# Low parts of two of the seven sum forms of g by a negative copy and an accumulating DMA, in the second FFN block of a float32 decoder step

## The chip, the cores and the metric

The kernel runs on one core of one Trainium2 chip. The metric is the device time of one execution in microseconds (us). All data are float32. A matmul here takes operands that are rounded to a shorter float format (fp32r), so every operand is cut into two parts, a high part (the rounded value) and a low part (the value minus its high part), and each product is built from three matmuls: high by high, high by low and low by high.

## What is computed

One step of a decoder block on 520 tokens (512 of a new sequence, 8 single-token samples): a SwiGLU FFN with half weight, a mixer (pooling and a state-space scan), a second SwiGLU FFN with half weight, and a final norm. The change lies in the second FFN alone:

```python
def _swiglu(x, wg, wu, wd):
    return (jax.nn.silu(x @ wg) * (x @ wu)) @ wd
...
    h = h + 0.5 * _swiglu(_rms_norm(h, ffn2_norm[l]), ffn2_w_gate[l], ffn2_w_up[l], ffn2_w_down[l])
```

The model width is 1024, the FFN width 2816, so the hidden vector g = silu(gate) * up has 22 tiles of 128 rows.

## The kernel before

**Tiles and products.** The FFN block is `class Ffn`. Both its matrix products, gate and up on one side and down on the other, are done as 2x2 block products with seven block multiplications in place of eight. The two token halves (260 tokens each) are one side of the blocks. Each of the seven forms of an input (sums and differences of its blocks, "slots" 0 to 6) is held as high and low part. One tile `f` of gate and up is one turn of seven products (`product(f, p)`), each of 12 matmuls: per 128-row piece one matmul with the high and one with the low part of the input against the high weight, and at the end four against the low weight (`mm_low_last`). So a turn has 84 matmuls.

**Where g goes.** The first 16 tiles of g are taken in pairs (0,1), (2,3), ... (14,15). When the odd tile of a pair is done, `keep_g` makes the seven forms of the pair in the tile `gs` (128 x 2 x 7 x 260, high parts in `gs[:,0]`, low parts in `gs[:,1]`) from `xg` (the four blocks, tile `gq`) and `xd` (two differences, which lie in the scratch `acc_f`). `part(hi, lo, s)` makes a cut: ScalarE casts to the high part, VectorE subtracts for the low part. Slots 0 to 2 come from `xg`, slots 3 and 4 from `xd` (the 128 x 520 cut in question), slots 5 and 6 from `xg` again after a further difference.

**Turns of the down weights.** After eight tiles of g there are four turns with down weights, `Down(c, d)` with d = 0 to 3: c = 0 follows tile 8 and uses pairs 0 to 3, c = 1 follows tile 16 and uses pairs 4 to 7. Their products read the forms in `gs`. A turn's products stand in the order 1, (product 4 of the turn before), 5, 6, 3, 7, 2. Product 1 reads slot 0, product 5 reads slot 3, product 7 slot 4. Each goes through the four pairs in order. The last pair that a Down turn needs, tiles (6,7) or (14,15), is closed one turn ahead of it, in the turn of tile 8 or 16.

**Low parts by DMA.** A second way to a low part already exists, `part_by_dma`: ScalarE casts to the high part, ScalarE writes the negative of the high part into the low part's place, and a DMA from the GpSimd queue adds the source to it. It is used for the low half-weights `wlo` and, by the table `LOW_BY_DMA`, for the last quarter of some tiles' up weights (`qs`). The other tiles' quarters are cut by VectorE.

**Order.** TensorE's order is pinned by hand. On the other engines a planner with a simulated timeline sets the order when the program is built, and each engine then runs its list in order. Weights come in by SyncE's DMA queue (`raw`, two pairs of 128 x 1024 buffers, one pair per turn). The GpSimd queue carries the accumulating DMAs and, between them, the 16 sample states (`br` and `room` in, `out_nss` out), whose update is done by ScalarE (`so`) and VectorE (`room`) in tiles 6 and 17 to 21 and in the Down turns.

In `product`, the copy of the first product's result out of PSUM into `BE` (ScalarE, L504) stands ahead of product 5, which writes the other half of the same `BE`.

Of the kernel before, what the change touches and what calls it, by code (L numbers as in the profile page):

```python
# [10 lines left out]
F32 = mybir.dt.float32  # L11
F32R = mybir.dt.float32r
AF = mybir.ActivationFunctionType
# [27 lines left out]
QUARTERS = slice(0, HB // 2), slice(HB // 2, HB)  # L41
STATES = ((1, 1, 1, 1), (6, 17, 19, 20, 21), 4)
OUT_LOW_BY_DMA = ((1, 0), (1, 1))
LOW_BY_DMA = {1: (2, 3, 4, 5, 6), 2: (*range(7), 9, 11)}

CONV_PLAN = (
    "b0 b1 d0 b2 b3 x0 x1 v0 d1 x2 x3 d2 X0 p0 y0 c0 A0 k0 p1 x4 m0 x5 B0 c1 p2 m1 A1 x6 c2 A2 B1 x7 X1 m2 A3"
# [21 lines left out]
def tile_trunk_step(ctx: ExitStack, tc: tile.TileContext, ins: dict, outs: dict):  # L69
    nc = tc.nc  # L70
# [172 lines left out]
                                              op1=ALU.subtract)  # L243

    def part_by_dma(hi, lo, s, home):
        nc.scalar.copy(hi, s)
        nc.scalar.activation(out=lo, in_=hi.bitcast(F32), func=AF.Copy, scale=-1.0)
        nc.gpsimd.dma_start(out=lo, in_=home, accum_op=ALU.add)

    def part(hi, lo, s):  # L250
        cast = nc.scalar.copy(hi, s)
        low = nc.vector.tensor_tensor(out=lo, in0=s, in1=hi.bitcast(F32), op=ALU.subtract)  # L252
        return cast.ins, low.ins
# [17 lines left out]
    class Ffn:  # L271
# [72 lines left out]
        def keep_g(self, f, tg):  # L344
            if f >= self.folded:
                if not self.few:
                    self.few = self.cells(f"g{self.i}_{f}")
                g = self.g[f] = self.few.pop().rearrange("p (a b) t -> p a b t", a=2)
                self.closed = part(g[:, 0], g[:, 1], tg)
                return  # L350
            self.g[f] = tg
            if f % 2:
                gs = self.gs[f // 2] = self.new_gs(f"gs{f}")
                xg, xd = self.pairs[f - 1], self.nx[2].rearrange("p (b t) -> p b t", b=2)
                nc.vector.tensor_tensor(out=xd, in0=xg[:, 0::2], in1=xg[:, 3:4].to_broadcast([P, 2, HB]),
                                        op=ALU.subtract)
                nc.vector.scalar_tensor_tensor(out=xg[:, 3], in0=xd[:, 1], scalar=-1.0, in1=xg[:, 0], op0=ALU.mult,
                                               op1=ALU.subtract)
                part(gs[:, 0, 0:3], gs[:, 1, 0:3], xg[:, 0:3])
                part(gs[:, 0, 3:5], gs[:, 1, 3:5], xd)  # L360
                nc.vector.scalar_tensor_tensor(out=xg[:, 2], in0=xg[:, 3], scalar=-1.0, in1=xg[:, 1], op0=ALU.mult,
                                               op1=ALU.subtract)
                part(gs[:, 0, 5:7], gs[:, 1, 5:7], xg[:, 2:4])
# [90 lines left out]
        def quarter(self, f):  # L454
            src = self.held[f]
            n = f"{self.i}_{f}b"
            if self.qs is None:
                hi, lo = (self.wx.tile([P, 512], F32R, tag=t, name=f"{t}_{n}") for t in ("qhi", "qlo"))
            else:
                hi, lo = self.qs[0][:, :512], self.qs[0][:, 512:]  # L460
            h, l = hi, lo
            if len(src.shape) == 3:
                h, l = (t.rearrange("p (j c) -> p j c", j=4) for t in (hi, lo))
            if f in LOW_BY_DMA[self.i] and (f, 1) not in LOW_ON_DVE:
                part_by_dma(h, l, src, self.dram[f][1][:, 512:])
            else:
                part(h, l, src)
            self.w[f][4] = (hi, lo), range(4)
# [1024 lines left out]
```

## Time and profile before

| | |
|---|---|
| time, median of 3 runs | 951.61 us (951.32 to 952.19) |
| the profiled execution | 952.73 us, of which the span on the core is 950.9 us |
| TensorE matmul / weight load busy | 941.6 us (99%) / 923.9 us (97%) |
| VectorE busy | 851.8 us (90%) |
| ScalarE busy | 635.7 us (67%) |
| GpSimd busy | 152.6 us (16%) |
| second block: tiles 1 to 21 and the eight Down turns | about 612 to 900 us of the span |

The span is the time from the first to the last instruction on the core; the profiled execution is 1.1 us slower than the median. Lines of the trace give a start in us from the span's start, a duration in us, the engine, the source line and the operation with its output and inputs. PE is TensorE, PEld its weight loads, DVE VectorE, ACT ScalarE, POOL GpSimd, SP SyncE; "POOLq" and "SPq" are their DMA queues. "Us to landing" of a DMA runs from its issue to the moment that its completion is signalled.

### The profile page before, as it was taken

Reading aid. Unit: us, or ns where it says so; the run is one execution under the profiler, and the core shown is the slowest. Engines: PE = TensorE matmul, PEld = TensorE weight load, DVE = VectorE, ACT = ScalarE, POOL = GpSimd, SP = SyncE. Lnnn points to the kernel's source line nnn. Section 1 sums busy time; section 2 is a strip of 40 time slices with the busy share of each in tenths; the row PEclk is TensorE's granted clock in tenths of the full one; section 3 lists DMA queues with packets and bytes.
Section 4 is the critical chain, followed back from the end, with each engine's and each line's share of the span. In section 5 each row is a group of like instructions: output and inputs, shape, how many; then the busy total and the mean of one; then the engine's idle time right before and its main releaser. Section 6 shows DMA issues by size and latency. Waiting matters only on the chain. (4 is left out here: it accounts for less than half of the span.)

```text
span 950.9 us, 19685 instructions
## 1 busy us (share of the span) xinstructions
PE 941.6 (99%) x7674; PEld 923.9 (97%) x7674; DVE 851.8 (90%) x1462; ACT 635.7 (67%) x1178; POOL 152.6 (16%) x230
## 2 busy tenths in 40 slices
PE   9999999999999999999999999999999999999996
PEld 8999999999999999999999899999999999999996
DVE  6899899998988698779998998999999999999986
ACT  7777756667566465475768745777776677766764
POOL 0011100100100002146251100111112101122120
PEclk9999999999999999999999999999999999999998
DMA  7666554455553335354364443546666655767642
GB/s 212 180 164 146 148 147 140 113 135 164 134 153 97 87 96 162 91 169 150 97 179 133 140 113 117 139 120 156 164 178 175 164 147 137 172 203 181 171 158 91
DMA packets 54123, 138.36 MB, mean 146 GB/s; under 512 B 7878, under 2 KB 16006, under 8 KB 54030
## 3 DMA queue, kind: packets, MB, share of 16 engines
q1 hardware_dynamic: 40046, 104.20, 34.6%
q0 software_dynamic: 13712, 32.78, 18.6%
q8 instruction: 60, 0.98, 0.4%
q14 instruction: 33, 0.27, 0.1%
q10 hardware_dynamic: 272, 0.13, 0.0%
HBM read 129.74 MB, written 7.34 MB: 144 GB/s over the span
## 5 line engine op out<-in xcount | busy, mean ns | idle before, releaser
L504 ACT COPY ac<-A 128x260 f32<-128x260 f32 x85 | 31.7, 373 | 34.6 <-PE A L165 16.4
L433 DVE TENSOR_TENSOR s<-raw 128x1024 f32<-128x1024 f32 x39 | 47.6, 1221 | 4.0 <-DMA raw<-in_w2gu 2.5
L504 ACT COPY ac<-BE 128x260 f32<-128x260 f32 x41 | 15.5, 377 | 33.4 <-PE BE L165 17.6
L151 PE MATMUL inx<-xh_mx,whi_inx 128*128 128x260 f32 x112 | 31.8, 284 | 0.0
L154 PE MATMUL inx<-xl_mx,whi_inx 128*128 128x260 f32 x112 | 31.6, 282 | 0.0
L155 PE MATMUL inx<-xh_mx,wlo_inx 128*128 128x260 f32 x112 | 31.6, 282 | 0.0
L1033 DVE SCALAR_TENSOR_TENSOR A<-U,h,A 128x544 f32<-128x544 f32 x36 | 28.4, 789 | 1.8 <-ACT A L1031 1.4
L311 PE MATMUL P<-x,raw 128*128 128x260 f32 x128 | 29.3, 390 | 0.0
L311 PEld LDWEIGHTS P<-x,raw 128*128 128x128 f32 x128 | 24.9, 196 | 3.9
L160 PE MATMUL wo<-catg,whi_wo 128*128 128x260 f32 x192 | 27.4, 285 | 0.0
L160 PEld LDWEIGHTS wo<-catg,whi_wo 128*128 128x128 f32 x192 | 24.8, 188 | 0.2
L139 ACT CAST thi<-raw 128x1024 fp32r<-128x1024 f32 (+1 forms) x14 | 14.2, 1014 | 15.5 <-PE wo L160 4.8
L1311 DVE TENSOR_TENSOR h<-wo,h 128x260 f32<-128x260 f32 x48 | 19.2, 423 | 4.9 <-PE wo L165 4.7
L1199 ACT ACTIVATE so<-br,sxdt 128x128 f32<-128x128 f32 x64 | 22.7, 375 | 1.2 <-DVE room L1201 0.7
L252 DVE TENSOR_TENSOR gs<-gq,gs 128x780 fp32r<-128x780 f32 (+1 forms) x28 | 23.2, 829 | 0.0
L151 PE MATMUL inz<-xh_mx,whi_inz 128*128 128x260 f32 x80 | 22.9, 287 | 0.0
L154 PE MATMUL inz<-xl_mx,whi_inz 128*128 128x260 f32 x80 | 22.7, 283 | 0.0
L155 PE MATMUL inz<-xh_mx,wlo_inz 128*128 128x260 f32 x80 | 22.6, 283 | 0.0
L512 DVE TENSOR_TENSOR BE<-BE,ac 128x260 f32<-128x260 f32 (+1 forms) x41 | 18.5, 451 | 3.1 <-PE BE L155 1.7
L151 PEld LDWEIGHTS inx<-xh_mx,whi_inx 128*128 128x128 f32 x112 | 21.1, 188 | 0.2 <-issue 0.2
L160 PE MATMUL A<-xth_f,qs 128*128 128x260 f32 x84 | 21.2, 283 | 0.0
L160 PE MATMUL A<-xtl_f,qs 128*128 128x260 f32 x84 | 21.2, 284 | 0.0
(3135 smaller groups left out, 4380.9 us busy)
## 6 DMA issues: line engine op xcount, KB each, us to landing
raw<-in_w2gu SPq DMA_DIRECT2D x44, 512.0 KB, 4.3
raw<-in_w1gu SPq DMA_DIRECT2D x41, 512.0 KB, 4.2
raw<-in_w_in SPq DMA_DIRECT2D x24, 512.0 KB, 3.6
raw<-in_w1d SPq DMA_DIRECT2D x16, 512.0 KB, 4.6
raw<-in_w2d SPq DMA_DIRECT2D x16, 512.0 KB, 4.3
raw<-in_w_out SPq DMA_DIRECT2D x12, 512.0 KB, 3.5
ab<-scr_acs SPq DMA_DIRECT2D x8, 512.0 KB, 6.3
h<-in_state_ssm SPq DMA_DIRECT2D x16, 256.0 KB, 3.7
```

The source lines that it names most:

```text
L151: first = nc.tensor.matmul(ps, whi, xhi, start=start, stop=False, **kw)
L154: nc.tensor.matmul(ps, whi, xlo, start=False, stop=False, **kw)
L155: nc.tensor.matmul(ps, wlo, xhi, start=False, stop=stop, **kw)
L160: mm = nc.tensor.matmul(ps, w, x, start=start, stop=False, **kw)
L252: low = nc.vector.tensor_tensor(out=lo, in0=s, in1=hi.bitcast(F32), op=ALU.subtract)
L311: mm = nc.tensor.matmul(self.banks[f, u][b][:, :HB], ws(self.raw[f][:, u], j + 4 * q), xg[:, slot[q]], start=j == q == 0, stop=j == 3 and ...
L433: nc.vector.tensor_tensor(out=s1, in0=diag, in1=up0, op=ALU.add)
L504: self.copied = nc.scalar.copy(keep, out[:, :HB]).ins
L512: nc.vector.tensor_tensor(out=be[:, s], in0=be[:, s], in1=a[:, s], op=ALU.add)
L1033: nc.vector.scalar_tensor_tensor(out=A[:, :n], in0=U[:, j : j + n], scalar=w(j), in1=A[:, :n], op0=ALU.mult, op1=ALU.add)
L1199: nc.scalar.activation(out=o[:, q], in_=br, func=AF.Copy, scale=sxdt[:, j, b : b + 1]))
L1311: rows.append(nc.vector.tensor_tensor(out=h[:, d, hs], in0=ps[:, :HB], in1=h[:, d, hs], op=ALU.add).ins)
```

## The change

```diff
-LOW_BY_DMA = {1: (2, 3, 4, 5, 6), 2: (*range(7), 9, 11)}
+LOW_BY_DMA = {1: (2, 3, 4, 5, 6), 2: (0, 1, 2, 3)}
...
     def part_by_dma(hi, lo, s, home):
-        nc.scalar.copy(hi, s)
-        nc.scalar.activation(out=lo, in_=hi.bitcast(F32), func=AF.Copy, scale=-1.0)
+        cast = nc.scalar.copy(hi, s)
+        low = nc.scalar.activation(out=lo, in_=hi.bitcast(F32), func=AF.Copy, scale=-1.0)
         nc.gpsimd.dma_start(out=lo, in_=home, accum_op=ALU.add)
+        return cast.ins, low.ins
...
                 part(gs[:, 0, 0:3], gs[:, 1, 0:3], xg[:, 0:3])
-                part(gs[:, 0, 3:5], gs[:, 1, 3:5], xd)
+                if self.i == 2:
+                    part_by_dma(gs[:, 0, 3:5], gs[:, 1, 3:5], xd, xd)
+                else:
+                    part(gs[:, 0, 3:5], gs[:, 1, 3:5], xd)
```

In the second block, slots 3 and 4 of each of the eight pairs get their low part by the negative copy on ScalarE and an accumulating DMA of 128 x 520 from `acc_f` in SBUF; VectorE's eight subtractions go. In return the last quarters of tiles 4, 5, 6, 9 and 11 (the new tuple drops all five, tiles 4 and 5 among them) are cut by VectorE and no longer by negative copy and DMA. In all VectorE has three instructions fewer, ScalarE three more, GpSimd's queue three DMAs more. TensorE's and SyncE's rows are the same ones in the same order. Line numbers from 247 on are higher by one in the new file, from 361 on by four.

The planner also places neighbours anew. On ScalarE the negative copies do not stand right behind their casts. This is ScalarE before, from the cast of slots 3 and 4 of pair (6,7) to the first copy of the turn Down(0,0); L396 casts the next turn's weights, L397 makes their negative copy:

```order
L251 CAST gs_8550<-acc_f_7244 128x520
L139 CAST shi_Down(c=0, d=0)d<-raw 128x1024
L504 COPY ac_8_1_8506<-A_8_8503 128x260
L1199 ACTIVATE so_8616<-br_8227,sxdt 128x128
L396 CAST whi_Down(c=0, d=1)a<-raw 128x1024
L251 CAST gs_8550<-gq_6_8427 128x520
L504 COPY BE_Down(c=0, d=0)_8646<-A_Down(c=0, d=0)_8645 128x260
L397 ACTIVATE wlo_Down(c=0, d=1)a<-whi_Down(c=0, d=1)a 128x1024
```

And ScalarE now, at the same place:

```order
L246 CAST gs_8550<-acc_f_7244 128x520
L139 CAST shi_Down(c=0, d=0)d<-raw 128x1024
L508 COPY ac_8_1_8506<-A_8_8503 128x260
L1203 ACTIVATE so_8617<-br_8227,sxdt 128x128
L247 ACTIVATE gs_8550<-gs_8550 128x520
L400 CAST whi_Down(c=0, d=1)a<-raw 128x1024
L252 CAST gs_8550<-gq_6_8427 128x520
L508 COPY BE_Down(c=0, d=0)_8647<-A_Down(c=0, d=0)_8646 128x260
L401 ACTIVATE wlo_Down(c=0, d=1)a<-whi_Down(c=0, d=1)a 128x1024
```

The negative copy (L247) stands three instructions behind its cast, between `so` and the cast of the next turn's weights. The same holds at Down(1,0).

On GpSimd's queue, before, from the low weights of tile 8 to those of Down(0,2):

```order
L398 DMA wlo_8a<-in_w2gu 128x512
L1179 DMA br_8613<-scr_bc 128x128
L1180 DMA room<-in_state_ssm 128x512
L398 DMA wlo_Down(c=0, d=0)a<-in_w2d 128x1024
L398 DMA wlo_Down(c=0, d=1)a<-in_w2d 128x1024
L1179 DMA br_8749<-scr_bc 128x128
L398 DMA wlo_Down(c=0, d=2)a<-in_w2d 128x1024
L1203 DMA out_nss<-room 128x512
```

And now:

```order
L402 DMA wlo_8a<-in_w2gu 128x512
L402 DMA wlo_Down(c=0, d=0)a<-in_w2d 128x1024
L248 DMA gs_8550<-acc_f_7244 128x520
L1183 DMA br_8614<-scr_bc 128x128
L1184 DMA room<-in_state_ssm 128x512
L402 DMA wlo_Down(c=0, d=1)a<-in_w2d 128x1024
L1183 DMA br_8750<-scr_bc 128x128
L1207 DMA out_nss<-room 128x512
L402 DMA wlo_Down(c=0, d=2)a<-in_w2d 128x1024
```

The new DMA stands ahead of a state's two loads, which have moved from in front of Down(0,0)'s low weights to behind it, so three transfers now come between Down(0,0)'s and Down(0,1)'s low weights. `out_nss` and Down(0,2)'s low weights have changed places. GpSimd's queue at Down(1,0) to Down(1,2) is altered in the same way.

## The prediction

> **What bounds the kernel now.** First the page's first part:
>
> ```profile
> span 950.9 us, 19685 instructions
> PE 941.6 (99%) x7674; PEld 923.9 (97%) x7674; DVE 851.8 (90%) x1462; ACT 635.7 (67%) x1178; POOL 152.6 (16%) x230
> ```
>
> TensorE leaves 1% of the span. Then the busy times in stretches of the second block (columns: stretch, length, then busy us and count of PE, PEld, DVE, ACT, POOL, the granted clock, DMA share, GB/s):
>
> ```profile
> 640.00:670.00 30.00, 30.00 (x250) 29.80 (x249) 27.49 (x43) 22.05 (x38) 6.31 (x8) 1.00 0.69 163
> 780.00:820.00 40.00, 40.00 (x334) 39.92 (x334) 38.12 (x61) 29.63 (x51) 4.60 (x6) 1.00 0.58 147
> ```
>
> TensorE never pauses long enough to be seen here, its clock is full, and VectorE at 92 to 95% only keeps step. A busy PE may still hide short gaps, so I read the chain that ended last:
>
> ```profile
> 771.34 0.97 PE A L160 x8
> 781.42 0.97 PE A L160 x8
> ```
>
> The same product of tiles 13 and 14 lies 10.08 us apart, which is 84 matmuls at 0.12 us. I went through the starts of all weight loads from tile 2 to the last Down turn in this way: only two gaps stand out, of 0.27 and 0.15 us. The first:
>
> ```profile
> 665.19 0.19 PEld L160 LDWEIGHTS A<-xtl_f,qs 128*128 128x128 f32 x1
> 665.58 0.54 PEld L165 LDWEIGHTS A<-xth_f,qs 128*128 128x128 f32 x4 [0.20 <-DMA qs<-in_w2gu]
> ```
>
> 0.39 us in place of 0.12: TensorE waited for the low quarter of tile 6 from an accumulating DMA. So the second block is bound by TensorE's own rate. Relief of VectorE can bring at most these 0.42 us there, but whatever makes TensorE wait is added to the end nearly one for one, since no slack follows in which to catch up.
>
> **The new wait.** The readers of slots 3 and 4 decide. For most pairs they come a turn or more later; for the last pair ahead of each Down group they come at once, in product 5:
>
> ```profile
> 696.35 1.03 PEld L160 LDWEIGHTS BE_Down(c=0, d=0)_8646<-gs,shi_Down(c=0, d=0)c 128*128 128x128 f32 x8
> 697.31 0.19 PEld L165 LDWEIGHTS BE_Down(c=0, d=0)_8646<-gs,slo_Down(c=0, d=0)c 128*128 128x128 f32 x1
> 817.29 1.02 PEld L160 LDWEIGHTS BE_Down(c=1, d=0)_10189<-gs,shi_Down(c=1, d=0)c 128*128 128x128 f32 x8
> 818.24 0.55 PEld L165 LDWEIGHTS BE_Down(c=1, d=0)_10189<-gs,slo_Down(c=1, d=0)c 128*128 128x128 f32 x4
> ```
>
> The eight loads take the pieces in order, high then low, so the eighth needs the low part of slot 3 of the last pair: at 696.35 + 7 x 0.12 = 697.19, and at 817.29 + 0.83 = 818.12. Before, VectorE had it ready long ago:
>
> ```profile
> 693.23 0.70 DVE L252 TENSOR_TENSOR gs<-acc_f,gs 128x520 fp32r<-128x520 f32 x1
> ```
>
> 693.93 leaves 3.3 us. Now it goes by ScalarE and GpSimd. ScalarE's rows there, for c = 0 and then c = 1:
>
> ```profile
> 693.35 0.37 ACT L1199 ACTIVATE so<-br,sxdt 128x128 f32<-128x128 f32 x1
> 693.66 1.05 ACT L396 CAST whi_Down(c=0, d=1)a<-raw 128x1024 fp32r<-128x1024 f32 x1
> 695.24 0.36 ACT L504 COPY BE_Down(c=0, d=0)_8646<-A_Down(c=0, d=0)_8645 128x260 f32<-128x260 f32 x1
> ...
> 814.43 1.05 ACT L396 CAST whi_Down(c=1, d=1)a<-raw 128x1024 fp32r<-128x1024 f32 x1
> 816.86 0.38 ACT L504 COPY BE_Down(c=1, d=0)_10189<-A_Down(c=1, d=0)_10188 128x260 f32<-128x260 f32 x1
> ```
>
> ScalarE runs without a pause here, so the negative copy behind `so` starts where the cast L396 started, at 693.66 and 814.43. Its length I take from the same operation on `qs`, and the step from ScalarE to GpSimd from tile 5:
>
> ```profile
> L247 ACT ACTIVATE qs<-qs 128x512 fp32r<-128x512 f32 x7 | 4.5, 636 | 0.2
> ...
> 643.64 0.64 ACT L397 ACTIVATE wlo_5a<-whi_5a 128x512 fp32r<-128x512 f32 x1
> ...
> 644.57 0.85 POOL L398 DMA_DIRECT2D wlo_5a<-in_w2gu  x1 [6.23 <-ACT wlo_5a L397]
> ```
>
> 0.64 us, and 644.28 to 644.57, 0.29 us. The DMA is issued at 693.66 + 0.64 + 0.29 = 694.59 and at 815.36; GpSimd is free at both places. With L for the time to landing, TensorE waits 694.59 + L - 697.19 = L - 2.60 at Down(0,0). At Down(1,0) I first take away the second gap of the trace: product 5 began at 817.29 because the copy into `BE` ended at 817.24; the new order puts that copy ahead of the 1.06 us negative copy of the weights and only the 0.64 us one of `gs` is new ahead of it, so it ends earlier and the gap of 0.15 goes. The need is then 817.97 and the wait L - 2.61.
>
> **What L is.** No accumulating DMA of before has its source in SBUF. The nearest rows are those from GpSimd's queue of nearly the same size (256 KB against 260; last column us to landing):
>
> ```profile
> qs<-in_w2gu POOLq DMA_DIRECT2D x7, 256.0 KB, 7.0
> ...
> out_nss<-hs POOLq DMA_DIRECT2D x3, 256.0 KB, 2.3
> ...
> wlo_5a<-in_w2gu POOLq DMA_DIRECT2D x1, 256.0 KB, 3.8
> ...
> wlo_7a<-in_w2gu POOLq DMA_DIRECT2D x1, 256.0 KB, 6.9
> wlo_8a<-in_w2gu POOLq DMA_DIRECT2D x1, 256.0 KB, 4.5
> ```
>
> The lower bound is 2.3, a plain copy out of SBUF; the upper one 7.0, an accumulate in a crowd. In between the neighbours decide. What else moves counts, so here are the raw loads that follow (SPq), first behind tile 5's issue at 644.57 above, then behind tile 8's, then at the two new places:
>
> ```profile
> 646.10 20.87 SPq L389 DMA_DIRECT2D raw<-in_w2gu  x6
> ...
> 675.56 0.85 POOL L398 DMA_DIRECT2D wlo_8a<-in_w2gu  x1 [7.11 <-ACT BE L504]
> ...
> 676.32 0.33 SPq L389 DMA_DIRECT2D raw<-in_w2d  x1
> ...
> 695.09 0.33 SPq L389 DMA_DIRECT2D raw<-in_w2d  x1
> ...
> 815.86 0.33 SPq L389 DMA_DIRECT2D raw<-in_w2d  x1
> ```
>
> Tile 5's 3.8 us had 1.5 us to itself, tile 8's 4.5 had 0.76; the new ones, issued at 694.59 and 815.36, have 0.5. I take L = 4.6, nearest to tile 8's row. Each wait is then 2.0 us, both 4.0; by the bounds the pair costs 0 (2.3 is under 2.60) to 8.8.
>
> The Trainium skill's page "DMA: Bandwidth & Descriptors", section "Anatomy of one DMA", gives a GpSimd DMA 2.0 us plus its bytes at 436 GB/s. For 266,240 bytes that is 2.6 us, an estimate from that page, and by it the sum would have no wait at all. The trace does not agree for accumulates of this size, 3.8 us even with the queue nearly to itself, though no run shows one out of SBUF.
>
> **The rest of the change.** VectorE loses 8 x 0.69 us and gains 5 x 0.68:
>
> ```profile
> L252 DVE TENSOR_TENSOR qs<-raw,qs 128x512 fp32r<-128x512 f32 x21 | 14.4, 683 | 0.0
> ...
> L252 DVE TENSOR_TENSOR gs<-acc_f,gs 128x520 fp32r<-128x520 f32 x8 | 5.5, 694 | 0.0
> ```
>
> That is 2.1 us less over 290 us beside a full TensorE, so 0; uncovered it would bring 2.1. The quarter of tile 6 now comes from VectorE and the 0.27 gap goes; with Down(1,0)'s 0.15, 0.42 us gained. ScalarE gets three negative copies more, 1.9 us, under an engine that is a quarter idle (22.05 of 30.00 above): 0, except where the copy into `BE` is close. At tile 3 it is:
>
> ```profile
> 634.69 0.38 ACT L504 COPY BE<-A 128x260 f32<-128x260 f32 x1
> ...
> 635.53 0.19 PEld L160 LDWEIGHTS BE<-xth_f,shi_3c 128*128 128x128 f32 x1
> ```
>
> The margin is 0.46 us, and a negative copy that shifts ScalarE by some 0.53 (the 636 ns overlap the next start a little) now stands ahead: 0.1 us lost. At Down(0,0) the margin of 0.75 holds. The swapped raw loads of tiles 6 and 7 arrive earlier in the half that ScalarE reads first; that gains nothing beyond the 0.42. DVE's next write of `acc_f` comes 10 us or more later, long after the DMA has read it: 0. Three more DMAs on GpSimd's queue, 0.86 us each there, hide in its idle time, but they push what stands behind. At Down(0,0) the low weights of Down(0,1) follow the new DMA and a state's two loads:
>
> ```profile
> 696.88 0.88 POOL L398 DMA_DIRECT2D wlo_Down(c=0, d=1)a<-in_w2d  x1 [10.30 <-PE A L165]
> ...
> 704.47 0.55 PEld L165 LDWEIGHTS A_Down(c=0, d=1)_8781<-gs,wlo_Down(c=0, d=1)a 128*128 128x128 f32 x4
> ...
> wlo_Down(c=0, d=1)a<-in_w2d POOLq DMA_DIRECT2D x1, 512.0 KB, 5.6
> ```
>
> It landed at 702.48, 2.0 us early. ScalarE is 0.54 later and up to 580 KB go ahead; if a share of that delays the landing by 2 to 3 us, TensorE, itself 2.0 later, still has about 0.5 to 1.5 us left. I count 0.
>
> **The sum.** 2.0 + 2.0 - 0.42 + 0.1 = +3.7 us on the profiled execution's 952.73, so 956.4. The median of the runs is 1.12 below that execution; for it I predict 951.61 + 3.7 = 955.3, 0.4% slower. Below 0.2% (1.9 us) a change can hardly be told from none here.
>
> **Rivals.**
>
> *The DMA lands in time.* It reads SBUF, not DRAM, and the only rows with that source land in 2.3 us. Up to L = 2.6 nothing waits, and the gaps that go leave 951.3, not slower; up to L = 3.6 the loss stays within 0.2%. For it speaks that row, and a pause in the DMA traffic, busy tenths of 690 to 700 in slices of 0.25 us:
>
> ```profile
> DMA  9979999830000000000000009949899503984698
> ```
>
> Nothing moves from 692.25 to 696. Against it, those three copies add nothing to a destination, lie in the quiet tail, and the raw load follows within 0.5 us. Chance 0.20. The formula of the Trainium skill above would give this case.
>
> *A queue that backs up.* L reaches 6 to 7 as in tile 7, or the pushed low weights of Down(0,1) and Down(0,2) come late as well, in both groups: two waits of 4.0 and two of 0.5 make +8.7, 960.3. For it speak the rows of 6.9 and 7.0; against it, the traffic of those had a second accumulate or an older load in the way. Chance 0.10.
>
> *VectorE's relief counts.* If the gaps I could not see were larger, the 2.1 us less of VectorE would come off at most: 949.5 without any new wait. TensorE's even step speaks against it. Chance 0.04.
>
> **How the numbers follow.** My case, two waits of 1.1 to 4.0 us each, has the remaining 0.66 and spans 953.5 to 959.3. The range takes in the rival that lands in time: 951.3 to 959.5. It leaves out the far end of the backing up, 0.10, and the relief, 0.04. Faster by over 0.2%: 0.03; within 0.2%: 0.21; slower: 0.76.
>
> **What the next profile would show.** If I am right, the chain of waits has TensorE waiting for a DMA named `gs<-acc_f` twice, at the eighth load of product 5 of Down(0,0) and of Down(1,0), by about 2 us each, the landing of `gs<-acc_f` has a median of 4 to 5 us, the wait for tile 6's `qs` is gone, and nearly all other turns still take 10.08 us. VectorE's busy time falls by about 2 us to no effect. I am wrong if TensorE's wait stands elsewhere (the copy into `BE`, low weights of a Down turn) or if those two loads run on without a gap.

## The result, and the profile after

| | before | after |
|---|---|---|
| time, median of 6 runs each, taken in turn | 951.81 us (951.02 to 952.86) | 958.14 us (956.04 to 960.84) |
| ratio after/before, 95% interval | | 1.0070 (1.0058 to 1.0082) |
| the profiled execution / its span | 952.73 / 950.9 us | 957.42 / 955.6 us |

The change makes the kernel 6.3 us slower. The prediction was 955.3 us, 3.7 us slower. The page of the changed kernel, the first part (busy us, share of the span, instructions):

```profile
span 955.6 us, 19713 instructions
PE 941.2 (98%) x7674; PEld 923.2 (97%) x7674; DVE 849.1 (89%) x1459; ACT 637.1 (67%) x1181; POOL 154.8 (16%) x233
```

VectorE has 2.7 us less work, and TensorE has the same work in a span 4.7 us longer. The two profiled executions do not reach the second block at the same time, so I compare the block alone. Here are the first weight load of tile 1's sums and the first load of `dhi_2d`, behind the block; before, then after (start us, us, engine, line, operation):

```profile
614.62 0.19 PEld L160 LDWEIGHTS BE<-xth_f,shi_1c 128*128 128x128 f32 x1
...
913.62 0.19 PEld L151 LDWEIGHTS dh<-g,dhi_2d 128*128 128x128 f32 x1
```
```profile
612.74 0.19 PEld L160 LDWEIGHTS BE<-xth_f,shi_1c 128*128 128x128 f32 x1
...
918.36 0.19 PEld L151 LDWEIGHTS dh<-g,dhi_2d 128*128 128x128 f32 x1
```

The block took 299.0 us and takes 305.6, which is 6.6 more. The 1.9 us by which the profiled execution came sooner to it is time from ahead of the change. Where the 6.6 us stand, the waits of TensorE's weight loads in and behind the block say (waiting line, what it waited for: us in total, times, longest):

```profile
PEld BE_Down(c=0, d=0)_8647 L160 <- DMA gs<-acc_f: 2.5, 1, 2.5
PEld BE_Down(c=1, d=0)_10192 L160 <- DMA gs<-acc_f: 2.4, 1, 2.4
PEld BE_Down(c=1, d=2)_10464 L160 <- ACT c_Down(c=1, d=2)_1_10466 L508: 0.9, 1, 0.9
...
PEld BE_Down(c=0, d=2)_8916 L160 <- ACT ac_Down(c=0, d=2)_1_8918 L508: 0.5, 1, 0.5
...
PEld A L160 <- ACT ac L508: 0.3, 1, 0.3
PEld A L165 <- DVE slo_18d L141: 0.2, 1, 0.2
```

That is 2.5 + 2.4 + 0.9 + 0.5 + 0.3 + 0.2 = 6.8, less the two old gaps of 0.42, which are gone: 6.4 us. The first two are the predicted waits. They stand where they were put, at the eighth load of product 5, behind seven loads that ran on:

```profile
694.42 0.90 PEld L160 LDWEIGHTS BE_Down(c=0, d=0)_8647<-gs,shi_Down(c=0, d=0)c 128*128 128x128 f32 x7
697.84 0.19 PEld L160 LDWEIGHTS BE_Down(c=0, d=0)_8647<-gs,shi_Down(c=0, d=0)c 128*128 128x128 f32 x1 [2.51 <-DMA gs<-acc_f]
```

**Why the landing took 5.1 us and not 4.6.** The DMA's issue and the next load of `raw` on SyncE's queue, and then the issues around Down(0,0) (KB each, median us to landing):

```profile
692.65 0.85 POOL L248 DMA_DIRECT2D gs<-acc_f  x1 [8.04 <-ACT gs L247]
```
```profile
692.53 0.33 SPq L393 DMA_DIRECT2D raw<-in_w2d  x1
```
```profile
raw<-in_w2d SPq DMA_DIRECT2D x2, 512.0 KB, 5.7
wlo_Down(c=0, d=1)a<-in_w2d POOLq DMA_DIRECT2D x1, 512.0 KB, 8.6
gs<-acc_f POOLq DMA_DIRECT2D x1, 260.0 KB, 5.1
```

The issue came as worked out: 692.65 and the 1.88 us of the earlier start make 694.53, against 694.59. But the raw load came 0.1 us ahead of it, where the prediction had it 0.5 us behind, from the place that it had before. It waits for VectorE to have read the old weights, and there the removed subtraction stood in front. Before (behind the row of 693.23 shown above), and after:

```profile
693.84 1.22 DVE L141 TENSOR_TENSOR slo_Down(c=0, d=0)d<-raw,shi_Down(c=0, d=0)d 128x1024 fp32r<-128x1024 f32 x1
```
```profile
691.29 1.22 DVE L141 TENSOR_TENSOR slo_Down(c=0, d=0)d<-raw,shi_Down(c=0, d=0)d 128x1024 fp32r<-128x1024 f32 x1
```

That row ended at 695.06 before, and the load was issued at 695.09; now it ends at 692.51, and the load is issued at 692.53. Against the block's start VectorE is 0.7 us earlier here, the subtraction of 0.70 us that went. So VectorE's relief did have an effect: it set off a 512 KB load into the one transfer that TensorE waits for.

**The waits that were not predicted.** ScalarE in Down(0,2) (and alike in Down(1,2)) has `so`, a step of the sample states, ahead of the copy of product 5's result out of PSUM, and product 3 cannot write until that is read. DVE's rows first, then ScalarE's:

```profile
716.37 1.23 DVE L437 TENSOR_TENSOR s_Down(c=0, d=3)_9037<-raw 128x1024 f32<-128x1024 f32 x1 [1.45 <-DMA raw<-in_w2d]
...
719.39 0.34 DVE L1205 SCALAR_TENSOR_TENSOR room<-room,sdec,so 128x128 f32<-128x128 f32 x1
```
```profile
719.76 0.37 ACT L1203 ACTIVATE so<-br,sxdt 128x128 f32<-128x128 f32 x1 [2.23 <-DVE room L1205]
720.07 0.37 ACT L508 COPY ac_Down(c=0, d=2)_1_8918<-BE_Down(c=0, d=2)_8916 128x260 f32<-128x260 f32 x1
```

A raw load comes 1.45 us late for VectorE, `room` is late behind it, `so` waits 2.23 us for `room`, and the copy that TensorE needs stands behind `so` in ScalarE's list. Before, the planner had the copy ahead of `so`. This is a change of order far from the edit.

### The profile page after: what moved, and what is told of

Same layout as the page of the kernel before. It is cut to its first block, busy times and chain, and to the rows that moved or that the text cites. A ratio compares the mean times of both kernels' runs of the same rounds, so it can differ in the third digit from the quotient of the medians.

```text
span 955.6 us, 19713 instructions
## 1 busy us (share of the span) xinstructions
PE 941.2 (98%) x7674; PEld 923.2 (97%) x7674; DVE 849.1 (89%) x1459; ACT 637.1 (67%) x1181; POOL 154.8 (16%) x233
## 4 chain that ended last, share of the span: by engine, by line
PE 39%; DVE 4%; DMA 3%; issue 2%; POOL 1%; ACT 1%; DVEq 0%; ACTq 0%
PE A L160 8%; PE BE L160 6%; PE wo L160 5%; PE A L165 4%; DMA raw<-in_w2d 3%; PE BE L165 3%; PE wo L165 2%; PE P L312 1%; PE dh L151 1%; PE dh L155 1%; PE dh L154 1%; POOL zs L1078 1%; PE inz L151 1%; PE inz L155 1%; PE inz L154 1%
## 5 line engine op out<-in xcount | busy, mean ns | idle before, releaser
L155 PEld LDWEIGHTS inx<-xh_mx,wlo_inx 128*128 128x128 f32 x112 | 21.1, 188 | 0.0
```

The source lines that it names most:

```text
L155: nc.tensor.matmul(ps, wlo, xhi, start=False, stop=stop, **kw)
```

## The experiments

Each kernel is the changed one with the edit shown, timed against the kernel before on the same chip. "Block" is the length of the second block in its profile less the 299.0 us of before.

| kernel | time, median | the kernel before there | ratio (95% interval) | median less before | block |
|---|---|---|---|---|---|
| the change | 958.14 | 951.81 | 1.0070 (1.0058 to 1.0082) | +6.3 | +6.6 |
| last pairs by VectorE | 953.04 | 951.18 | 1.0016 (1.0006 to 1.0026) | +1.9 | +1.4 |
| last pairs only by DMA | 956.12 | 951.18 | 1.0051 (1.0037 to 1.0065) | +4.9 | +5.6 |
| quarters only | 953.50 | 951.18 | 1.0022 (1.0012 to 1.0031) | +2.3 | +1.8 |
| order 2, 6, 5, 3, 7 | 953.87 | 951.18 | 1.0030 (1.0020 to 1.0040) | +2.7 | +2.8 |
| state called later | 958.67 | 951.04 | 1.0080 (1.0066 to 1.0093) | +7.6 | +8.4 |
| order 2, 6, 5, 7, 3 | 955.77 | 951.04 | 1.0053 (1.0040 to 1.0067) | +4.7 | +5.2 |
| quarters as before | 959.62 | 951.04 | 1.0091 (1.0076 to 1.0105) | +8.6 | +8.9 |
| the two above together | 956.42 | 951.04 | 1.0055 (1.0042 to 1.0068) | +5.4 | +5.8 |
| negative copy at once | 953.23 | 951.14 | 1.0024 (1.0015 to 1.0032) | +2.1 | +2.2 |
| the same, order 2, 5, 6, 3, 7 | 954.09 | 951.14 | 1.0034 (1.0021 to 1.0047) | +3.0 | +3.6 |
| negative copy twice | 958.64 | 951.14 | 1.0077 (1.0064 to 1.0090) | +7.5 | +7.7 |
| DMA in two | 955.12 | 951.14 | 1.0042 (1.0028 to 1.0056) | +4.0 | +4.3 |

The last two columns agree within 0.8 us in all rows, so the time is made or lost in this block, by what makes TensorE pause.

### Which part of the change costs

**Last pairs by VectorE.** Only the two urgent pairs, tiles (6,7) and (14,15), go back to the subtraction.

```diff
-                if self.i == 2:
+                if self.i == 2 and f not in (7, 15):
```

> The changed kernel, but the last pair ahead of each Down group (tiles 6,7 and 14,15) has its low part of slots 3 and 4 cut by VectorE again; the other six pairs stay with the negative copy and the DMA. Late landing (TensorE waits 2.5 us twice for the DMA of these two pairs): both waits go, and since the planner's order at Down(0,2) and Down(1,2) is that of before too, 951.3 to 952.8 us. Rival, the added DMAs crowd the queues: six of eight are still there, so most of the 6 us loss stays, 955 or more. Rival, the quarters' moves or the planner's new order in tiles 3 to 21 cost time: 954 or more.

Measured +1.9 us, 4.5 less than the change and just above the theory's 952.8. Both waits for `gs` are gone and `so` stands behind the copy again. With the subtraction back, the raw load is back in its old place too: it is issued at 693.79, 80.4 us behind the block's start, where it was 80.5 before and 79.8 in the change. What is left is another order on ScalarE, at Down(1,0):

```profile
816.08 1.06 ACT L401 ACTIVATE wlo_Down(c=1, d=1)a<-whi_Down(c=1, d=1)a 128x1024 fp32r<-128x1024 f32 x1
817.04 0.37 ACT L508 COPY BE_Down(c=1, d=0)_10190<-A_Down(c=1, d=0)_10189 128x260 f32<-128x260 f32 x1
```

The copy into `BE` stands behind a 1.06 us negative copy, and TensorE waits 1.3 us for it. In the change the copy is ahead.

**Last pairs only by DMA**, the other six by VectorE:

```diff
-                if self.i == 2:
+                if self.i == 2 and f in (7, 15):
```

> The changed kernel, but only the last pair ahead of each Down group has its low part by DMA; the other six pairs are cut by VectorE. Late landing: both waits of about 2.5 us stay and so does ScalarE's order at Down(0,2) and Down(1,2) in which the state's instruction stands ahead of the PSUM copy: 956 to 959 us. Rival, crowded queues: with two of eight DMAs left most of the loss goes, 953 or less.

```profile
PEld A L160 <- DVE gq L559: 1.7, 2, 1.3
PEld BE_Down(c=1, d=0)_10186 L160 <- DMA gs<-acc_f: 1.6, 1, 1.6
PEld BE_Down(c=0, d=0)_8644 L160 <- DMA gs<-acc_f: 1.5, 1, 1.5
PEld A_Down(c=0, d=1)_8779 L165 <- DMA wlo_Down(c=0, d=1)a<-in_w2d: 0.8, 1, 0.8
```

Measured +4.9, at the lower end of the theory, but with waits of 1.5 and 1.6 us and not of 2.5. Here the raw load is issued 0.8 us behind the new DMA (694.57 and 693.74), which lands in 4.2 us:

```profile
gs<-acc_f POOLq DMA_DIRECT2D x1, 260.0 KB, 4.2
```

Two more things come to light. Where the wait for `gs` is shorter, the low weights pushed behind it are late (0.8 us). And VectorE is late by 1.3 us at tile 6, where it now cuts the quarters as well.

**Quarters only**, all pairs by VectorE (no FFN block has the number 3):

```diff
-                if self.i == 2:
+                if self.i == 3:
```

> Only the second half of the change: the quarters of tiles 4, 5, 6, 9 and 11 by VectorE, all eight pairs by VectorE as before. Late landing: no DMA to wait for, the wait for tile 6's quarter gone, 951.0 to 952.5 us. This kernel has ScalarE's new order at Down(0,2) and Down(1,2) as well, the state's instruction ahead of the PSUM copy; if that order alone makes TensorE wait, 952.5 to 953.5. Rival, VectorE's extra work in tiles 4 to 11 makes it late: 953.5 or more, with waits of TensorE for VectorE in these tiles.

```profile
PEld A L160 <- DVE gq L559: 1.0, 1, 1.0
PEld BE_Down(c=1, d=2)_10456 L160 <- ACT c_Down(c=1, d=2)_1_10458 L508: 1.0, 1, 1.0
```

Measured +2.3: 1.0 us for VectorE at tile 6, and `so` ahead of the copy in Down(1,2). So the quarters by themselves are not free for VectorE. In the whole change no wait for VectorE stands at tile 6: the subtractions that went made the room. VectorE's relief was spent, not wasted.

**Order 2, 6, 5, 3, 7** of the products in Down(0,0) and Down(1,0) only, so that product 5 comes 2.9 us later (the condition is shown shortened):

```diff
-for k, p in enumerate((2, 5, 6, 3, 7) if t in (2, KF - 1) else (5, 6, 3, 7, 2)):
+for k, p in enumerate((2, 5, 6, 3, 7) if t in (2, KF - 1) else (2, 6, 5, 3, 7)
+                      if self.i == 2 and t in ((0, 0), (1, 0)) else (5, 6, 3, 7, 2)):
```

> The changed kernel, but in Down(0,0) and Down(1,0) the products stand in the order 1, 4 of the turn before, 2, 6, 5, 3, 7, so that slot 3 is read 2.9 us later; all DMAs as in the changed kernel. Late landing: the wait of 2.5 us twice is covered by other products, 951.5 to 953.5 us, with no wait of TensorE for gs. Rival, crowded queues or VectorE and ScalarE late: the loss does not hang on where slot 3 is read, 956 or more.

```profile
PEld BE_Down(c=0, d=0)_8647 L160 <- ACT ac_Down(c=0, d=0)_1_8649 L508: 1.5, 1, 1.5
PEld BE_Down(c=1, d=0)_10192 L160 <- ACT c_Down(c=1, d=0)_1_10194 L508: 1.4, 1, 1.4
```

Measured +2.7. The waits for `gs` are gone and so is the bad place of `so`, which shows that they made most of the loss. But product 3 now stands right behind 5 and writes the same `BE`: it waits 1.5 and 1.4 us for the copy of 5's result.

### Can the waits be taken away one by one?

**State called later.** In Down(0,2) and Down(1,2) the sample state's step is called behind product 5, queued behind its copy:

```diff
-                for _ in range(STATES[0][t.d] if ...):
+                late = self.i == 2 and t in ((0, 2), (1, 2))
+                for _ in range(0 if late else STATES[0][t.d] if ...):
...
+                    if p == 5 and late:
+                        with queued(self.copied):
+                            next(self.states, None)
```

> The change, with the sample state of the turns Down(0,2) and Down(1,2) called behind product 5 instead of at the head of the turn, so that ScalarE's `so` stands behind the copy of product 5's result again. Theory (two separate terms, the landing and ScalarE's order): the two waits for the DMA `gs<-acc_f` stay at 2.4 to 2.5 us each, TensorE's waits of 0.5 and 0.9 us for ScalarE in those two turns go, the time is 1.4 us under the change's: the kernel before + 4.9, about 956.5. Rival (the late raw load is what costs, and TensorE only meets it at another place when ScalarE's order is changed): no gain, before + 6.3, about 958.

Measured +7.6: no gain, so the theory fell in its number. The waits of 0.5 and 0.9 us did go, but ScalarE meets the late step elsewhere: in tile 17 `so` now waits for its own late load, and the copy into `BE` behind it makes TensorE wait 1.0 us.

```profile
863.42 0.66 ACT L1207 ACTIVATE so<-br,sxdt 128x128 f32<-128x128 f32 x2 [1.07 <-DMA br<-scr_bc]
864.02 0.61 ACT L401 ACTIVATE wlo_18a<-whi_18a 128x512 fp32r<-128x512 f32 x1
864.54 0.37 ACT L508 COPY BE<-A 128x260 f32<-128x260 f32 x1
```

Another 1.5 us of this profile are matmuls at half rate, of which more below.

**Order 2, 6, 5, 7, 3**, so that product 7 stands between 5 and 3 (the edit is shown against the kernel with the order 2, 6, 5, 3, 7):

```diff
-                      (2, 6, 5, 3, 7) if self.i == 2 and ...
+                      (2, 6, 5, 7, 3) if self.i == 2 and ...
```

> The change, with the products of Down(0,0) and Down(1,0) in the order 2, 6, 5, 7, 3 instead of 5, 6, 3, 7, 2: product 5 comes 24 matmuls (2.88 us) later, and product 7 stands between 5 and 3. The planner's order on ScalarE then has `so` behind the copy in Down(0,2) and Down(1,2). Theory (all of the loss is waits): the waits for `gs<-acc_f` (2.5 us) are covered, the wait of product 3 for the copy of product 5's result (1.4 to 1.5 us when 3 stood right behind 5) is covered by the 1.44 us of product 7, the waits of 0.5 and 0.9 us go; tile 3's 0.3 us stays and the old gaps of 0.42 us stay away: the kernel before + 0 within 0.5, 950.7 to 951.7. Rival (more transfers on GpSimd's queue make the pushed low weights of Down(0,1) and Down(1,1) late as soon as TensorE no longer waits for `gs`): 0.8 us twice, before + 1.6, about 952.8. Rival (the wait only moves on, as it did with the order 2, 6, 5, 3, 7): before + 2.7, about 953.9.

Measured +4.7, more than the theory and both rivals had. The wait for `gs` is gone, but product 7 waits 0.8 and 1.1 us for ScalarE's other copy, and the planner's new order costs up to 1.6 us at a place in tiles 18 and 19:

```profile
PEld A L160 <- ACT ac L508: 1.8, 2, 1.6
PEld A_Down(c=1, d=0)_10191 L160 <- ACT c_Down(c=1, d=0)_0_10193 L508: 1.1, 1, 1.1
PEld BE L160 <- ACT BE L508: 0.9, 1, 0.9
```

**Quarters as before**, with the low parts of `gs` by DMA in all pairs:

```diff
-LOW_BY_DMA = {1: (2, 3, 4, 5, 6), 2: (0, 1, 2, 3)}
+LOW_BY_DMA = {1: (2, 3, 4, 5, 6), 2: (*range(7), 9, 11)}
```

> The new low parts of g's slots 3 and 4 alone: the quarters of tiles 4, 5, 6, 9 and 11 go by negative copy and DMA as before. `so` still stands ahead of the copy in Down(0,2) and Down(1,2). Theory (the quarters by VectorE cost nothing of their own beside the other half of the change; what they cost alone came from VectorE being short of time there): waits for `gs<-acc_f` of 2.4 to 2.5 us twice, 0.5 and 0.9 us for ScalarE, and the old 0.3 us gap at tile 6's quarter back: before + 6.6, about 958.2. Rival (the quarters by VectorE cost their 2 us inside the change too): before + 4.5, about 956.

Measured +8.6: to take the quarters' move back saves nothing. TensorE's gaps add up to 6.1 us more than before, near the theory's 6.6, against 6.7 in the change, with both waits for `gs` (2.8 and 2.5 us); matmuls at half rate behind them make the other 2.8. **The two together** (this and the order 2, 6, 5, 7, 3):

> The new low parts of slots 3 and 4, the quarters as before, and the products of Down(0,0) and Down(1,0) in the order 2, 6, 5, 7, 3. Theory: no wait for `gs<-acc_f`, `so` behind the copy, tile 6's old gap of 0.3 us and tile 3's 0.3 us: before + 0.4, 951.2 to 952. VectorE has 5.5 us less work than in the kernel before, which by this theory brings nothing, since TensorE's rate sets the end. Rival (VectorE's relief counts once nothing waits for the DMA): up to 5.5 us faster, any time clearly under before - 1, so under 950.

Measured +5.4, so the theory fell and so did the rival. VectorE has 5.7 us less work than before (846.1 us busy in the kernel without the new order) and nothing comes of it; the waits are those of the order, and the low weights of Down(0,1) and Down(1,1) are late by 1.2 and 0.4 us.

### The cause itself

**Negative copy at once.** ScalarE's negative copy stood behind a 1.05 us cast and `so`. Here these two are told to stand behind it:

```diff
-                    part_by_dma(gs[:, 0, 3:5], gs[:, 1, 3:5], xd, xd)
+                    self.neg = part_by_dma(gs[:, 0, 3:5], gs[:, 1, 3:5], xd, xd)[1]
...
-            e2 = split(s2, 1024, f"{n}d", wx, 2, ("shi", "slo"))
+            with queued(*((self.neg,) if i == 2 and f in ((0, 0), (1, 0)) else ())):
+                e2 = split(s2, 1024, f"{n}d", wx, 2, ("shi", "slo"))
...
-                    next(self.states, None)
+                    with queued(*((self.neg,) if self.i == 2 and t in ((0, 0), (1, 0)) else ())):
+                        next(self.states, None)
```

> The change, with ScalarE's negative copy of the last pair's slots 3 and 4 placed ahead of the cast of Down(c,0)'s sums and of `so` (by telling the planner that these two stand behind it); the rest of ScalarE's order, and `so` ahead of the copy in Down(0,2) and Down(1,2), nearly as in the change. The copy then ends about 1.26 us sooner (0.95 for the cast, 0.31 for `so`, from the change's rows), and the next load of `raw`, which comes behind the subtraction that follows the moved cast, starts later, so that the DMA has the queues to itself for longer. Theory (the wait is set by when the DMA is issued and by the raw load beside it): the two waits for `gs<-acc_f` fall from 2.5 to between 0 and 0.5 us, no half-rate stretch of TensorE follows, the waits for `so` of 0.5 and 0.9 us stay or grow by up to 0.9 each: the kernel before + 1.2 to + 3.2, 952.2 to 954.2. Rival (the DMA's landing, however early, is bound by something else on its queue): waits of over 1.2 us stay, before + 4 or more.

```profile
PEld A_Down(c=0, d=1)_8782 L165 <- DMA wlo_Down(c=0, d=1)a<-in_w2d: 1.1, 1, 1.1
PEld A_Down(c=1, d=1)_10330 L165 <- DMA wlo_Down(c=1, d=1)a<-in_w2d: 1.1, 1, 1.1
```
```profile
wlo_Down(c=0, d=1)a<-in_w2d POOLq DMA_DIRECT2D x1, 512.0 KB, 7.8
gs<-acc_f POOLq DMA_DIRECT2D x1, 260.0 KB, 3.3
```

Measured +2.1, inside what the theory said, and 4.2 less than the change. Issued sooner and with the raw load 2.8 us behind, `gs` lands in 3.3 us and nobody waits for it. The waits of 0.5 and 0.9 us are gone too, though ScalarE's list still has `so` ahead of the copy. In Down(0,2):

```profile
717.96 0.37 ACT L1205 ACTIVATE so<-br,sxdt 128x128 f32<-128x128 f32 x1 [0.96 <-DVE room L1207]
718.34 0.38 ACT L509 COPY ac_Down(c=0, d=2)_1_8918<-BE_Down(c=0, d=2)_8916 128x260 f32<-128x260 f32 x1
```

`so` waits 0.96 us for `room` in place of 2.23, and the copy comes in time. VectorE does not wait for a raw load there this time. So in these two kernels the order costs something only where a load that `room` stands behind is late as well. What is left was hidden by the first wait: the low weights of Down(0,1) and Down(1,1) land in 7.8 us in place of the 5.6 of before, 1.1 us late each.

**The same, order 2, 5, 6, 3, 7:**

> The same, and the products of Down(0,0) and Down(1,0) in the order 2, 5, 6, 3, 7, so that product 5 comes 1.44 us later. The planner's order then has `so` behind the copy of product 5's result in Down(0,2) and Down(1,2). Theory (all of the loss is these waits): no wait for `gs<-acc_f`, none of the 0.5 and 0.9 us; tile 3's 0.3 us stays and the old gaps stay away: the kernel before + 0 to + 1, 951 to 952. Rival (any change of ScalarE's order opens another wait of about 1 us, as in the two kernels that moved products by two places): before + 2 to + 4. Rival (VectorE's 2 us of relief counts once the waits are gone): before - 1 or less.

```profile
PEld A_Down(c=0, d=0)_8646 L160 <- ACT ac_Down(c=0, d=0)_0_8648 L509: 1.4, 1, 1.4
PEld A_Down(c=1, d=1)_10330 L165 <- DMA wlo_Down(c=1, d=1)a<-in_w2d: 0.9, 1, 0.9
PEld A_Down(c=1, d=0)_10191 L160 <- ACT c_Down(c=1, d=0)_0_10193 L509: 0.7, 1, 0.7
```

Measured +3.0: worse than without it. The rival was right that a new order of ScalarE opens other waits.

**Negative copy twice**, to make the wait longer (the new last argument of `part_by_dma` repeats the negative copy):

```diff
-                    part_by_dma(gs[:, 0, 3:5], gs[:, 1, 3:5], xd, xd)
+                    part_by_dma(gs[:, 0, 3:5], gs[:, 1, 3:5], xd, xd, 2 if f in (7, 15) else 1)
```

> The change, with the negative copy of slots 3 and 4 of the two last pairs done twice (the same values again), which holds the DMA back by about 2.1 us (from the change's rows: the second copy stands behind the 1.04 us cast of the weights and the 0.63 us cast of `gs`). It asks what a longer wait of TensorE costs beyond itself. Theory (the granted clock falls to 0.50 for some 3.4 us when a stretch of the clock's own windows lies mostly in a wait, as in the two kernels whose waits of 2.6 to 2.9 us were followed by matmuls at half rate): the waits become 4.5 to 4.7 us, each is followed by at least 3.4 us at a clock of 0.50, which costs 1.7 us more each: before + 6.3 + 4.2 + 2 to 3.4, 963.5 to 965, mean clock 0.994 or less in every run. Rival (the half-rate stretches have another cause than the wait's length): before + 6.3 + 4.2, about 961.5, the mean clock as scattered as in the change (0.994 to 0.997).

```profile
694.66 0.85 POOL L249 DMA_DIRECT2D gs<-acc_f  x1 [10.04 <-ACT BE_Down(c=0, d=0)_8648 L509]
```
```profile
gs<-acc_f POOLq DMA_DIRECT2D x1, 260.0 KB, 3.3
```

Measured +7.5; the wait did not grow from 2.5 us, and the theory and its rival were both wrong on that. What a longer wait costs therefore stays open. The DMA was issued 2.0 us later than in the change, at 694.66 in place of 692.65, and landed only 0.2 us later, since by then the raw load was on its way out: 3.3 us in place of 5.1. The landing has no length of its own; the issue and the raw load set it together. By the time of the raw load's issue less that of the DMA, the landings are 3.3 us at -2.1 (here), 5.1 at -0.1 (the change), 4.2 at +0.8 (last pairs only by DMA) and 3.3 at +2.8 (negative copy at once).

**DMA in two**, slot 3 first:

```diff
-                    part_by_dma(gs[:, 0, 3:5], gs[:, 1, 3:5], xd, xd)
+                    nc.scalar.copy(gs[:, 0, 3:5], xd)
+                    nc.scalar.activation(out=gs[:, 1, 3:5], in_=gs[:, 0, 3:5].bitcast(F32), func=AF.Copy, scale=-1.0)
+                    for q in range(2):
+                        nc.gpsimd.dma_start(out=gs[:, 1, 3 + q], in_=xd[:, q], accum_op=ALU.add)
```

> The change, with the accumulating DMA of slots 3 and 4 issued as two of 128 x 260, slot 3 first; product 5 needs slot 3 alone. It asks what the 5.1 us of the landing beside a raw load are made of. Theory (bytes that share the queues with the raw load): half the bytes land sooner, the waits fall from 2.5 to between 0.8 and 1.6 us, before + 3 to + 4.6. Rival (a fixed time from issue to the completion signal): the waits stay at 2.2 to 2.5 us, before + 5.8 to + 6.6, about 957.

```profile
PEld BE_Down(c=0, d=0)_8651 L160 <- DMA gs<-acc_f: 1.9, 1, 1.9
PEld BE_Down(c=1, d=0)_10200 L160 <- DMA gs<-acc_f: 1.8, 1, 1.8
```

Measured +4.0, inside the theory's time, but by another way: the waits lie between the two forecasts, and the waits for the copies behind `so` in Down(0,2) and Down(1,2) have shrunk to 0.2 and 0.3 us. Half the bytes shorten the wait by 0.6 us of 2.5, so most of the landing does not go by the bytes of this transfer.

## Why the prediction was right, and where it was off

- **TensorE bounds the block, and a wait is added nearly one for one.** Right: in all thirteen kernels the gaps between TensorE's weight loads (with the half rate told of below) add up to the block's growth within 0.2 us, and 5.7 us less work on VectorE brought nothing.
- **Two waits at the eighth load of product 5.** Right in place, number and reader. Mis-sized: 2.0 us each were predicted, 2.5 and 2.4 measured, since L was 5.1 and not 4.6. The step that failed took the raw load from its old place; the removed subtraction moved it 0.7 us forward, to the DMA's side. For the 0.5 us that the prediction assumed, L itself was well chosen: between the landings of 5.1 at -0.1 and 4.2 at +0.8 a straight line gives 4.5, an estimate from these two rows.
- **The two old gaps go, 0.42 us.** Right: neither stands among the waits after. (SyncE's rows carry the same names in the same order, but by the kernels' programs the loads of gate and up weights have changed places in tiles 6, 7 and also 11; after the change no wait of TensorE stands at these tiles.)
- **The copy into `BE` at tile 3, 0.1 us.** 0.3 us measured, and at the copy `ac` out of PSUM that stands just ahead of it on ScalarE; the negative copy pushes that as well, and I had taken the margin of the second one only.
- **ScalarE's reorders cost 0 elsewhere.** Wrong: 0.5 and 0.9 us in Down(0,2) and Down(1,2). The new order has `so` there ahead of the copy, and the prediction looked for such a step only at the turns with the new DMA and at tile 3. With a late load ahead of `room`, this is most of what the sum lacked (1.4 us; the two mis-sized waits are 0.9, tile 3 is 0.2, and a wait for `slo_18d`, which the prediction did not have, is 0.2). By the prediction's own sign, a wait of TensorE at another place, it was wrong here. That the time still lies within the width left for L is luck as far as these terms go.
- **VectorE's 2.1 us are worth 0.** Right in sum (2.7 us measured), but by another way than said. The subtractions that went pay for the quarters (alone these make TensorE wait 1.0 us for VectorE at tile 6), and they bring the raw load forward.
- **The pushed low weights, 0.** Right in the change, where the wait for `gs` hides them; with that wait gone they cost 1.1 us twice, so the rival that the queue backs up had the right mechanism in its second half.
- **The rival that the DMA lands in time**, which the estimate of 2.6 us from the Trainium skill's page "DMA: Bandwidth & Descriptors", section "Anatomy of one DMA", would give, fell: the landing takes 3.3 us with the raw load 2.8 us behind, in the negative copy at once, and 5.1 beside a raw load. One reading for it was wrong as well: the rows of 2.3 us are not the only copies out of SBUF. The same view of the kernel before has thirteen more of that size, from `room`, with a median of 5.0 us:

```profile
out_nss<-room POOLq DMA_DIRECT2D x13, 256.0 KB, 5.0
```

No kernel here beats the one before.

## What to carry over

Where the bounding engine has no slack, a cheaper way to make an operand must be judged at its most urgent reader: here six pairs of eight had time and two had not. When work is taken off an engine, look at what that engine releases next; the transfer that it sets off sooner can land on the very one that is waited for. And where a planner orders the rest, read its whole new order for steps that moved ahead of a copy the bounding engine needs.

## What the runs showed of the hardware that was not expected

A wait of TensorE can cost more than its length. In the kernel with the quarters as before, the second block in stretches of 1 us (stretch, length, busy us of PE, PEld, DVE, ACT, POOL, then the granted clock, DMA share, GB/s):

```profile
696.00:697.00 1.00, 0.00 (x0) 0.00 (x0) 1.00 (x4) 0.16 (x2) 0.79 (x1) 1.00 1.16 251
...
698.00:699.00 1.00, 0.63 (x3) 0.64 (x4) 0.38 (x2) 0.00 (x0) 0.00 (x0) 0.50 1.35 119
...
700.00:701.00 1.00, 1.00 (x7) 1.00 (x6) 0.00 (x0) 0.97 (x4) 0.00 (x0) 0.50 0.87 201
...
702.00:703.00 1.00, 1.00 (x10) 1.00 (x9) 0.03 (x1) 0.41 (x2) 0.00 (x0) 1.00 1.00 291
```

Before a wait of 2.8 us is over the clock falls to 0.50, and until it rises again TensorE's weight loads follow one another every 0.217 us in place of 0.12. (The counts of the view take in every instruction that touches a stretch, so they do not give this rate.) By the trace's record of the granted clock it fell at 697.865 and rose at 701.278, and again at 824.158 and 827.572: 3.41 us each time, and also in the two other profiles that show it (state called later, 699.97 to 703.39; negative copy twice, 699.42 to 702.83). At half rate that costs some 1.5 us. The two falls in one run are 126.30 us apart, 37 times 3.41, and in each of the fourteen traces all changes of the clock, up to the last fall at the end of the span, lie a whole number of 3.413 us apart. So the clock changes at the ends of fixed stretches of that length, wherever the waits lie.

Which waits make it fall then hangs on how the ends cut them. In the stretches ahead of the four falls TensorE had no weight load for 2.05 to 2.44 us. The other four waits of 2.4 us and more, two of them the changed kernel's own, are cut in two by the end of a stretch; no stretch there has more than 1.81 us without a weight load, and the clock did not fall. The uncut waits of 1.9 us in "DMA in two" come to 1.86 us and did not make it fall either. This bound holds for this block alone: at the end of the span, where the smaller matmuls of the final norm run, the clock falls behind stretches with as little as 0.9 us without a weight load.

The Trainium skill, page "TensorE: Matmul & The Clock Gate", section "What's actually happening", has such a free-running window of 3413 ns and a half rate; the trace agrees in both. The same page's rule, in "Why this matters for your kernels", that idle gaps up to about 3 us are safe is too generous here: 2.5 us were enough.

The change's own profiled execution has no such stretch, but its runs differ in mean clock: 0.996 to 0.997 at 956.0 to 958.2 us, 0.995 and 0.994 at 960.0 and 960.8. The kernel before had 0.996 to 0.998 in 50 runs, as had all kernels whose waits stayed under 2 us; the four with waits of 2.4 us and more went down to 0.993 to 0.995 in some runs. So the change's two slowest runs may hold such stretches, but no profile of them shows it. The mean clock alone does not give the time either: in "negative copy twice" the runs at 0.993 took 958.10 and 958.72 us, and those at 0.996 took 958.46 to 958.69.
